# Second half of a convolution: transposes for its statistics a product later, two groups of weight sums gated at another place

## The chip, the cores and the metric

The kernel runs on one core of one Trainium2 chip. Its time is the device time of one execution in microseconds (us); the time of a kernel is the median of several executions. Engines are named as in the profile: PE (TensorE, its matmuls), DVE (VectorE), ACT (ScalarE), POOL (GpSimd) and SP (SyncE, which here only issues DMAs).

## The reference, cut to what matters

1024 tokens of 1024 channels pass two layers. Layer 0 mixes tokens with a gated linear recurrence, layer 1 with a causal Conformer convolution; each mixer is followed by a squared-ReLU MLP of 4096 hidden units, with a residual and a layer norm after each. The change lies in layer 1:

```python
def conformer_conv_mixer(h, w_pw1, b_pw1, w_dw, b_dw, ln_g, ln_b, w_pw2, b_pw2):
    u = h @ w_pw1 + b_pw1
    a, gate = jnp.split(u, 2, axis=-1)
    u = a * jax.nn.sigmoid(gate)
    u = depthwise_causal_conv(u, w_dw) + b_dw            # 31 taps per channel
    u = jax.nn.silu(layer_norm(u, ln_g, ln_b))
    return u @ w_pw2 + b_pw2
x = layer_norm(ALPHA * x + mix, ln_mix_g[1], ln_mix_b[1])
ff = jnp.square(jax.nn.relu(x @ ffn_w1[1])) @ ffn_w2[1]
x = layer_norm(ALPHA * x + ff, ln_ffn_g[1], ln_ffn_b[1])
```

## The kernel before, in words

**Products.** Every matrix is held as two float32r parts, hi and lo, with hi + lo the float32 value. `product` (L327) issues three matmuls per block of 128 input channels (hi·hi, hi·lo, lo·hi), so a product over 1024 channels is 24 matmuls of 128x512. At its end it runs one entry of the list `bg.chores` and then `bg.pump`, which hands out background work (the convolution's taps) to DVE and POOL, as far as a clock of estimated costs lets it. A scheduler then fixes the order of the instructions on every engine from a timing model; on the chip each engine takes its instructions in that order, and the SP queue its DMAs too. A weight comes as a raw tile by DMA; ACT copies it to hi, DVE subtracts to get lo (`Slots.split`, L76); `wa.ahead(n)` keeps up to n weights ready.

**Order of layer 1.** The tokens are cut in two halves of 512. The string `SEQ` (L38) gives the steps: P is the first pointwise product with gate, N the end of a half's convolution, F its norm and SiLU, S the second pointwise product with residual and norm (`second`, L1322), UA and UB the first MLP product of the first and the second half (`up_half`), V, W and X parts of the two last column sets of that product, Z the rest of these. While the second half is convolved (18 taps on DVE into a PSUM bank, 12 on POOL through products made by ACT), PE works at UA0 to UA3 and V6. F1 is spread over UA4 and UA5, S1 follows, then W6, X7 and UB0 to UB5. From V6 to W6 two PSUM banks are left for products (L1405), S1's among them.

**Statistics of the second half.** The convolution's result stays channel by channel: `by_channel(j)` is a 128x512 tile of channel block j. Its norm needs sums over channels, so after every odd j `measured` (L1207) transposes blocks j-1 and j on PE (8 transposes of 128x128 into two PSUM banks) and DVE takes `bn_stats` of them. `convolve` appends `measured` to the list `late` at the end of block j (L1234) and empties `late` at tap 10 of the next block (L1197 to L1199). The last `measured` is run by `stats` in `second_half` (L1268), which then calls `averages` (L1255): `bn_aggr` four times, plus eps on DVE, power -1/2 on POOL (L1260), minus mean times scale on DVE. A chore later `spread` (L1273) multiplies scale and minus-mean-times-scale, each broadcast, by the identity on PE, so that they lie along the free dimension in two PSUM banks. DVE then multiplies each of the eight channel blocks by the scale, POOL adds the other (L1284), ACT and DVE make SiLU and split it into `sT[1]` (the tile `xb`), which S1 multiplies. As the blocks of a pair are done, their space takes the residual back by DMA (L1296, `kept` into `y`); `second` scales it by ALPHA and adds a bias on DVE (`y<-y,b_pw`).

**Weight sums.** The MLP of layer 1 multiplies in seven forms of 2x2 blocks where there would be eight products, so some weights are sums of the four blocks of a column set. `pool_sums` (L443) loads the four blocks into a ring of four raw tiles, makes four sums on POOL (128x1024 each, every one from the one before it) and stores each to DRAM by an SP DMA. With an argument `after`, POOL first copies one column of `after` into each tile: the loads then can't start before `after` is written.

Of the kernel before, what the change touches and what calls it, by code (L numbers as in the profile page):

```python
# [8 lines left out]
F32 = mybir.dt.float32  # L9
# [6 lines left out]
P = 128  # L16
D = 1024
S = 1024
KB = D // P
# [241 lines left out]
def body(ctx, tc, d, out):  # L261
# [21 lines left out]
    def ring(kbs, shape, name, dt=F32):  # L283
        return Ring([view(kb, shape, dt, name) for kb in kbs])

    def run(kb, n, size):
        return [kb + i * size for i in range(n)]
# [4 lines left out]
    def raws(kbs, name="raw"):  # L292
        return ring(kbs, (1024,), name)

    def bank(ids):
        return Ring([banks[:, i] for i in ids])
# [18 lines left out]
    bg = Background()  # L315
# [8 lines left out]
    def aux():  # L324
        return rings["aux"]().rearrange("p (a b) -> p a b", a=NTB)
# [112 lines left out]
    def sum_place(name, layer, c):  # L438
        if (name, layer, c) not in sums:
            sums[name, layer, c] = dram.tile([4, P, 1024], F32, name=f"sum_{name}{layer}{c}")  # L440
        return sums[name, layer, c]

    def pool_sums(name, layer, c, four, after=None):  # L443

        t = sum_place(name, layer, c)
        a = {q: four() for q in (2, 3, 0, 1)}
        for q in a:
            if after is not None:
                nc.gpsimd.tensor_copy(out=a[q][:, :1], in_=after)
            nc.sync.dma_start(out=a[q], in_=d[name][layer, c, q])  # L450

        for i, (x, y) in zip((1, 0, 2, 3), ((2, 3), (0, 2), (3, 0), (0, 1))):
            nc.gpsimd.tensor_tensor(out=a[y], in0=a[x], in1=a[y], op=ALU.add)
            nc.sync.dma_start(out=t[i], in_=a[y])

    to_sum = [(*of, c) for of in (("w2", 0), ("w2", 1)) for c in range(NFC)]
# [44 lines left out]
    qn, kn, at = ([p1(n) for _ in range(2)] for n in ("qn", "kn", "at"))  # L501
# [188 lines left out]
    def half_stats(bs, yt, j):  # L690
        vector.bn_stats(bs[:, j], yt[:, j * HT : (j + 1) * HT])
# [400 lines left out]
    x2T, sT, x3T = [xa, xb], [xa, xb], [xa, None]  # L1092
# [44 lines left out]
    cs, conv, pooled, late = [None, None], [], [], []  # L1137
# [26 lines left out]
    def tap(j, i):  # L1164
        return par[:, TAP + j * TAPS + i : TAP + j * TAPS + i + 1]
# [19 lines left out]
    def by_channel(j):  # L1185
        return ct[1][:, j // 2, j % 2 * HT : (j % 2 + 1) * HT]

    def convolve(half, j, u, sums, other):

        while half > normed[0]:  # L1190
            yield WAIT
        ca = cvs()
        if gate[1]:
            nc.vector.tensor_copy(out=ca[:, :1], in_=gate[1].pop())
        nc.scalar.activation(ca, u[:, :HT], AF.Identity, bias=par[:, BDW + j : BDW + j + 1], scale=tap(j, 0))  # L1195
        for i in range(1, TAPS - NPOOL):
            if i == (10 if half else 6):  # L1197
                while late:
                    late.pop(0)()  # L1199
            vector.scalar_tensor_tensor(out=ca, in0=u[:, i : i + HT], scalar=tap(j, i), in1=ca, op0=ALU.mult, op1=ALU.add)  # L1200
            yield
        bg.flush(other)
        cb = sums["cb"]
        vector.tensor_tensor(out=by_channel(j) if half else cb, in0=ca, in1=cb, op=ALU.add)
        yield

        def measured():  # L1207

            if j == 1:
                cs[1] = stat.tile([P, NTB, 4, 6], F32, tag="cs", name="cs", bufs=1)  # L1210
            for t in range(0, NTB, 2):
                pt = rings["aux"]().rearrange("p (a b) -> p a b", a=2)
                for a in range(2):
                    for b in range(2):
                        tensor.transpose(pt[:, a, b * P : (b + 1) * P], by_channel(j - 1 + b)[:, (t + a) * P : (t + a + 1) * P], ident)
                for a in range(2):
                    vector.bn_stats(cs[1][:, t + a, j // 2], pt[:, a])

        def back():
            pt = aux()  # L1220
            for t in range(NTB):
                tensor.transpose(pt[:, t, :], cb[:, t * P : (t + 1) * P], ident)
            nc.scalar.copy(out=ct[half][:, :, j * P : (j + 1) * P], in_=pt)
            turned[0] += 1
            if j % 4 == 3:
                if j == 3:
                    cs[half] = stat.tile([P, NTB, 4, 6], F32, tag="cs", name="cs", bufs=1)[:, :, :2]
                for t in range(NTB):
                    half_stats(cs[half][:, t], ct[half][:, t, :], j // 4)

        if half:
            turned[0] += 1
        if half == 0 or j % 2:
            late.append(measured if half else back)  # L1234
# [29 lines left out]
    def second_half():  # L1264

        at = {}

        def stats():  # L1268
            while late:
                late.pop(0)()  # L1270
            at["mv"] = averages(1)

        def spread():  # L1273

            for i, name in ((3, "scale"), (4, "mean")):
                at[name] = pt = banks[:, (3, 7)[i - 3]]
                for t in range(NTB):
                    tensor.matmul(pt[:, t * P : (t + 1) * P], at["mv"][:, t, i : i + 1].to_broadcast([P, P]), ident, start=True, stop=True)
            m = big("z")
            nc.scalar.copy(out=m, in_=at["mean"])  # L1280
            for j in range(KB):
                c = by_channel(j)
                vector.tensor_tensor(out=c, in0=c, in1=at["scale"], op=ALU.mult)
                nc.gpsimd.tensor_tensor(out=c, in0=c, in1=m, op=ALU.add)  # L1284

            pool_sums(*to_sum.pop(0), raws((144, 148, 152, 161), "four"))

        def one(j):
            c, sg = by_channel(j), big("r")
            gj, bj = par[:, CLG + j : CLG + j + 1], par[:, CLB + j : CLB + j + 1]  # L1290
            nc.scalar.activation(sg, c, AF.Sigmoid, bias=bj, scale=gj)
            nc.scalar.activation(c, c, AF.Identity, bias=bj, scale=gj)
            vector.tensor_tensor(out=c, in0=c, in1=sg, op=ALU.mult)
            split(sT[1][:, 0, j, :], sT[1][:, 1, j, :], c)
            if j % 2:
                nc.sync.dma_start(out=ct[1][:, j // 2, :], in_=kept[1][j // 2])  # L1296

        nothing = lambda: None
        bg.chores += [stats, spread, nothing, *(lambda j=j: (one(j), one(j + 1)) for j in range(0, KB, 2))]

    def finish(half):
# [188 lines left out]
    for op, i in steps:  # L1490

        if op + str(i) in ("P10", "S0", "S1", "UA0", "UB0", "Z0"):
            bg.done()

        bg.hold = op in ("N", "F", "S") or bg.hold and op == "P1"
        if op == "S":
            gate[:] = sT[i][:, 1, KB - 1, :1].bitcast(F32), [ct[i][:, NTB - 1, :1]] * 2
            wa.behind = [gate[0]] * (3 if i == 0 else 0)
        bg.margin = 1e3 if op == "S" else 5.0 if op in ("N", "F") else 0.0 if op != "P1" else bg.margin
        if op in ("P0", "P1"):  # L1500
            pointwise(int(op[1]), i)
        elif op == "N":
            normalise(i)
        elif op == "F":
            if i == 1:

                rings["aux"] = bank((0, 4, 3, 7))
            second_half() if i else finish(i)
        elif op == "S":
            second(i)  # L1510
        elif op == "UA":
            up_half(1, i, 0, wa, stA, x3T[0])
        elif op in AHEAD:
            late_ahead(i, AHEAD[op])
        elif op == "Z":
            late_rest()
        else:
            if i == 0:
                wa.raws = raws((184, 188))
                drop(wa_last[1])  # L1520

                four = raws((132, 136, 140, 216), "four")
                for c in range(LATE):
                    pool_sums("w1b", 0, c, four, x3T[1][:, 1, KB - 1, 3 * P - 1 : 3 * P].bitcast(F32))
                wa.plan([form("w1b", 0, c, j) for j in LATE_ORDER for c in range(LATE)])
                stB = {"hr": ring(run(0, 2, 16), (8, 2, 256), "hb"), "r": ring(run(128, 2, 2), wide_t, "r"), "t": ring(run(112, 4, 4), (2, 2, 256), "ht")}
            if i == 2:
                x4 += ring((132, 136, 140, 216), (2, HT), "x4", F32R).views
                tmp = ring(run(176, 4, 2), wide_t, "xt")
                for k in range(4):  # L1530
                    bg.chores += x3_differences(k, tmp)
            up_half(1, i, 1, wa, stB, x3T[1])
# [98 lines left out]
```

Two calls matter here. In `spread` (L1286) a set of `w2` is summed, with no `after`. At UB0 (L1522 to L1525) the two late sets of `w1b` are summed in the same four tiles one after the other, with `after` a column of the lo part of `x3T[1]` (the tile `xc`, the normed input of UB): the last channel block, last token of token block 2 of the four that `second` makes by `norm` and `turn` (one `norm` and eight transposes per token block, then two hi and two lo splits).

## Time and profile before

| | before |
|---|---|
| median of 3 executions | 2132.28 us (2131.18 to 2132.79) |
| profiled execution, its own time | 2131.32 us |
| span of the profile | 2129.5 us |
| outside the span | 1.82 us |
| PE granted clock, mean | 0.999 |
| DMA read and written | 364.73 MB and 184.55 MB, 258 GB/s over the span |

Times in the profile count from the start of the span. A row of the timeline has start, length, engine, line of the code, operation, output and inputs, and how many equal instructions in a row it merges; in brackets the idle time before it and what ended that. Line L196 is the wrapper that all matmuls and most DVE and POOL operations go through, so operations are told apart by their tiles. The waits view has, after the colon, total us, times and the longest one.

### The profile page before, as it was taken

The numbers are of one execution on the slowest core, as the hardware profiler recorded it, in microseconds if no ns is written. First come the engines' busy times: TensorE is split into PE (matmuls) and PEld (weight loads), VectorE is DVE, ScalarE is ACT, GpSimd is POOL, SyncE is SP. The second block draws the span as 40 slices with busy tenths as digits, with TensorE's granted clock in tenths as the row PEclk, the third lists the DMA queues.
The fourth block names the chain that finished last, engine by engine and source line by source line (L and its number), as shares of the span: only waits on it lengthen the run. The fifth ranks groups of instructions, "written<-read, shape, count | busy, mean of one in ns | idle before, by whom it ended". The sixth has DMA issues, their size and how long they took to land. (4 is left out here: it accounts for less than half of the span.)

```text
span 2129.5 us, 27331 instructions
## 1 busy us (share of the span) xinstructions
PE 2108.3 (99%) x10136; PEld 1753.2 (82%) x10136; DVE 1534.3 (72%) x2208; ACT 971.4 (46%) x1370; POOL 451.5 (21%) x405
## 2 busy tenths in 40 slices
PE   8999999999999999999999999999999999999998
PEld 7888888888888888888888888888788888888887
DVE  7568898877777666656666798799957946765456
ACT  4222332232266555544444676557444445534333
POOL 0001121123100000000001599189513200040002
PEclk9999999999999999999999999999999999999999
DMA  5567867854248767899998755564585997996642
GB/s 185 144 159 175 229 178 180 232 157 176 92 144 295 268 229 258 310 372 325 339 337 308 292 193 183 208 247 168 194 299 196 335 349 263 370 341 219 192 163 99
DMA packets 166118, 500.76 MB, mean 235 GB/s; under 512 B 15840, under 2 KB 45792, under 8 KB 164704
## 3 DMA queue, kind: packets, MB, share of 16 engines
q1 hardware_dynamic: 159264, 473.85, 63.1%
q0 software_dynamic: 6720, 25.17, 6.7%
q8 instruction: 79, 1.29, 0.2%
q14 instruction: 55, 0.45, 0.1%
HBM read 364.73 MB, written 184.55 MB: 258 GB/s over the span
## 5 line engine op out<-in xcount | busy, mean ns | idle before, releaser
L196 PE MATMUL ps<-dw,dh 128*128 128x512 f32 x2688 | 611.0, 389 | 0.0
L196 PEld LDWEIGHTS ps<-dw,dh 128*128 128x128 f32 x2688 | 504.1, 188 | 104.5
L196 PE MATMUL ps<-x1f,fw 128*128 128x512 f32 x1344 | 305.3, 389 | 0.0
L196 PEld LDWEIGHTS ps<-x1f,fw 128*128 128x128 f32 x1344 | 252.1, 188 | 52.3
L196 PE MATMUL ps<-xa,wa 128*128 128x512 f32 x1152 | 267.5, 391 | 0.0
L196 PEld LDWEIGHTS ps<-xa,wa 128*128 128x128 f32 x1152 | 214.5, 188 | 44.4 <-ACT r L932 0.3
L196 POOL TENSOR_TENSOR cb<-cb,prod 128x512 f32<-128x512 f32 x176 | 234.2, 1340 | 17.8 <-ACT prod L1180 7.1
L196 DVE TENSOR_TENSOR dw<-dr,dw 128x1024 fp32r<-128x1024 f32 x112 | 141.4, 1264 | 97.2 <-ACT dw L77 94.2
L196 DVE TENSOR_TENSOR dh<-dh 128x1024 fp32r<-128x1024 f32 x112 | 140.4, 1256 | 93.7 <-ACT dh L77 93.5
L196 DVE SCALAR_TENSOR_TENSOR ps<-u,par,ps 128x512 f32<-128x512 f32 x288 | 199.6, 752 | 10.9 <-ACT ps L1195 9.4
L196 PE MATMUL ps<-x0T,wa 128*128 128x512 f32 x768 | 189.5, 399 | 6.2 <-ACT x0T L375 6.2
L77 ACT CAST dw<-dr 128x1024 fp32r<-128x1024 f32 x112 | 117.5, 1053 | 156.8 <-PE ps L196 133.8
L77 ACT CAST dh<-dh 128x1024 fp32r<-128x1024 f32 x112 | 117.1, 1050 | 124.9 <-DMA dh<-hf 124.3
L196 PEld LDWEIGHTS ps<-x0T,wa 128*128 128x128 f32 x768 | 142.9, 190 | 35.2 <-ACT x0T L375 6.2
L77 ACT CAST wa<-raw 128x1024 fp32r<-128x1024 f32 (+1 forms) x75 | 76.8, 1026 | 174.4 <-PE ps L196 118.2
L196 PE MATMUL ps<-xc,wa 128*128 128x512 f32 x672 | 153.3, 389 | 0.5 <-DVE wa L196 0.5
L1180 ACT ACTIVATE prod<-u,par 128x512 f32<-128x512 f32 x176 | 125.5, 722 | 56.3 <-POOL cb L196 55.6
L196 PEld LDWEIGHTS ps<-xc,wa 128*128 128x128 f32 x672 | 126.0, 188 | 27.5 <-DVE wa L196 1.3
L196 PE MATMUL ps<-wv,x0T 128*128 128x512 f32 x576 | 140.5, 395 | 0.0
L196 DVE TENSOR_TENSOR wa<-raw,wa 128x1024 fp32r<-128x1024 f32 (+1 forms) x75 | 96.9, 1293 | 58.4 <-ACT wa L77 54.6
L411 POOL TENSOR_TENSOR mv<-mv,nhalf 128x1 f32<-128x1 f32 x32 | 45.6, 1425 | 405.2 <-DVE mv L196 405.2
L196 PEld LDWEIGHTS ps<-wv,x0T 128*128 128x128 f32 x576 | 106.2, 188 | 21.4
(223 smaller groups left out, 2775.7 us busy)
## 6 DMA issues: line engine op xcount, KB each, us to landing
wa<-ready SPq DMA_DIRECT2D x122, 512.0 KB, 4.8
dh<-hf SPq DMA_DIRECT2D x112, 512.0 KB, 5.1
ready<-spare SPq DMA_DIRECT2D x74, 512.0 KB, 4.8
dr<-sum_w SPq DMA_DIRECT2D x64, 512.0 KB, 7.1
sum_w<-in_w_dram SPq DMA_DIRECT2D x24, 1024.0 KB, 8.9
dr<-in_w_dram SPq DMA_DIRECT2D x48, 512.0 KB, 7.6
hf<-ht SPq DMA_DIRECT2D x80, 256.0 KB, 4.1
raw<-in_w1q_dram SPq DMA_DIRECT2D x36, 512.0 KB, 4.0
```

What stands on the lines that cost most here:

```text
L77: self.nc.scalar.copy(out=slot[:, 0, c], in_=raw[:, c])
L196: return op(*args, **kw)
L411: nc.gpsimd.tensor_tensor(out=dst, in0=src, in1=nhalf[:, :n], op=ALU.pow)
L1180: nc.scalar.activation(tp, u[:, k : k + HT], AF.Copy, scale=tap(j, k))
```

## The change

Three edits.

1. At tap 10 of a block of the second half, `late` is not run but moved to the end of `bg.chores`; `product` runs it at its next end, so `measured` is issued one product later.
2. The `pool_sums` of `spread` gets `after = at["mv"][:, 0, 3:4]`, the scale that POOL's power has just made.
3. The `pool_sums` of the late sets at UB0 take as `after` the last token of token block 1 of `xc` in place of block 2.

```diff
             if i == (10 if half else 6):
+                if half:
+
+                    bg.chores += late
+                    late.clear()
                 while late:
                     late.pop(0)()
...
-            pool_sums(*to_sum.pop(0), raws((144, 148, 152, 161), "four"))
+            pool_sums(*to_sum.pop(0), raws((144, 148, 152, 161), "four"), at["mv"][:, 0, 3:4])
...
-                    pool_sums("w1b", 0, c, four, x3T[1][:, 1, KB - 1, 3 * P - 1 : 3 * P].bitcast(F32))
+                    pool_sums("w1b", 0, c, four, x3T[1][:, 1, KB - 1, 2 * P - 1 : 2 * P].bitcast(F32))
```

The program that is built from it has the same instructions on PE, DVE and ACT, and four more copies of one column on POOL.

## The prediction

> **What bounds the kernel now.** First the page: its engines and its chain.
>
> ```profile
> span 2129.5 us, 27331 instructions
> PE 2108.3 (99%) x10136; PEld 1753.2 (82%) x10136; DVE 1534.3 (72%) x2208; ACT 971.4 (46%) x1370; POOL 451.5 (21%) x405
> PE 20%; DVE 0%; DVEq 0%; issue 0%
> ```
>
> PE is busy for all but 21.2 us of the span, and no matmul is added or removed, so only PE's idle time can be won or enlarged. Next the view of waits, for PE, then the timeline of PE round each wait behind 1400 us.
>
> ```profile
> PE ps L196 <- ACT x0T L375: 6.2, 1, 6.2
> PE ps L196 <- DVE y L196: 3.0, 2, 1.9
> ...
> PE ps L196 <- DVE wa L196: 0.5, 2, 0.3
> ```
> ```profile
> 1474.55 28.14 PE L196 MATMUL ps<-xa,wa 128*128 128x512 f32 x123
> 1504.64 0.88 PE L196 MATMUL ps<-ident,y 128*128 128x128 f32 x6 [1.95 <-DVE y L196]
> ...
> 1535.96 1.16 PE L196 MATMUL ps<-ident,mv 128*128 128x128 f32 x8 [0.46 <-POOL mv L1260]
> 1538.29 1.16 PE L196 MATMUL ps<-ident,mv 128*128 128x128 f32 x8 [1.17 <-DVE mv L196]
> ...
> 1686.20 11.18 PE L196 MATMUL ps<-xc,wa 128*128 128x512 f32 x48 [0.32 <-DVE wa L196]
> 1697.55 12.80 PE L196 MATMUL ps<-xc,wa 128*128 128x512 f32 x55 [0.18 <-DVE wa L196]
> ```
>
> The largest wait (6.2) is at the kernel's start. Where the change works, PE loses 1.95 us before transposes of the statistics, 0.46 + 1.17 = 1.63 us before the matmuls that spread mean and scale, and 0.32 + 0.18 = 0.50 us in the UB steps. That is 4.08 us, or 0.19%: all that can be won. A wait made new on the path can cost more.
>
> **Part 1: transposes a product later.** Gain taken: **0**. What is issued later need not stand later, since a scheduler orders PE. Comparing the two built orders: each `measured` was split into two transposes and, later, six; counted in matmuls of UA0 to V6, the six stood behind numbers 79, 196 and 349, and in the changed program they stand behind 79, 196 and 349 again. Only the first two, which read the earlier block, go back (from 24 to 48, from 105 and 107 to 120, from 220 and 226 to 240). The 1.95 us is that of the six behind number 349; what ends it is the last add of block 5:
>
> ```profile
> 1503.91 0.68 DVE L196 TENSOR_TENSOR y<-ps,cb 128x512 f32<-128x512 f32 x1
> ```
>
> DVE's order is the same up to there, so the add ends at 1504.59 and the wait stays. Bounds: 0 to 1.95 won; I take 0, because the order says so.
>
> **Part 2: the sums of `w2` gated by the scale.** Gain: **1.63**. POOL and DVE before:
>
> ```profile
> 1530.05 4.87 POOL L453 TENSOR_TENSOR four<-four 128x1024 f32<-128x1024 f32 x2 [20.81 <-DVE cs L196]
> 1534.88 1.03 POOL L1260 TENSOR_TENSOR mv<-mv,nhalf 128x4 f32<-128x4 f32 x1
> 1541.60 12.33 POOL L1284 TENSOR_TENSOR y<-y,z 128x512 f32<-128x512 f32 x8
> ```
> ```profile
> 1531.02 1.46 DVE L196 TENSOR_SCALAR mv<-mv 128x4 f32<-128x4 f32 x1
> 1535.94 2.29 DVE L196 SCALAR_TENSOR_TENSOR mv<-mv 128x4 f32<-128x4 f32 x1 [3.46 <-POOL mv L1260]
> ```
>
> The power had its input at 1532.48 but stood behind two weight sums until 1534.88. The tiny DVE instruction behind it then took 2.29 us, as long as the weight sum that POOL had begun at its side. In the changed order POOL has the power, four one-column copies, one sum, two `y<-y,z`, a sum, six `y<-y,z`, two sums. The power ends near 1533.5 at the latest and DVE's instruction meets copies alone, so both are done before PE arrives at 1535.5. Both waits go.
>
> What is late next is S1. The four loads now leave at 1532.5 or later, so the first sum, ahead of every `y<-y,z`, starts near 1538 to 1540 (5.1 to 7.3 us behind the copies, by rows of part 3) and ends near 1541 to 1542: the first `y<-y,z` comes when it did (1541.60). The second sum delays the last six by about 2.5 us, and the last two sums now run at the side of DVE's SiLU products, which POOL slows:
>
> ```profile
> 1551.00 3.48 DVE L196 TENSOR_TENSOR y<-y,r 128x512 f32<-128x512 f32 x2
> 1563.27 1.29 DVE L196 TENSOR_TENSOR y<-y,r 128x512 f32<-128x512 f32 x2
> 1564.64 1.30 DVE L196 TENSOR_TENSOR xb<-y,xb 128x512 fp32r<-128x512 f32 x2
> 1565.97 1.23 DVE L196 SCALAR_TENSOR_TENSOR y<-y,b_pw 128x1024 f32<-128x1024 f32 x1
> 1570.56 1.22 DVE L196 SCALAR_TENSOR_TENSOR y<-y,b_pw 128x1024 f32<-128x1024 f32 x1 [3.37 <-DMA y<-kept]
> 1575.80 0.69 DVE L196 TENSOR_TENSOR y<-y,ps 128x512 f32<-128x512 f32 x1 [4.02 <-PE ps L196]
> ```
> ```profile
> 1567.44 39.84 PE L196 MATMUL ps<-wa,xb 128*128 128x512 f32 x175
> ```
>
> 1.74 us each with POOL at work, 0.65 without. With POOL busy to about 1562 in place of 1554, some four such instructions lose 1.1 us each, so the last split of `xb` ends near 1570.5, not 1565.94. S1 (1.63 earlier: 1565.8) reads the last two channel blocks in its matmuls 31 to 36, from 1572.6 at 39.84 / 175 = 0.228 us each: in time. But the last `kept` load leaves only after that split and its residual was ready 4.6 us later (1565.97 to 1570.56), so `y<-y,b_pw` ends near 1576.4, where 4.02 us of slack stood before `y<-y,ps`. S1 has two PSUM banks; `y<-y,ps` (0.69) must have read the first before matmul 49, at 1576.8, and now ends at 1577.1 if four DVE instructions are slowed, at 1579.3 if six are. With three there would be no wait: 0 to 2.5 us, and I take **+0.7**. On SP the stores of the sums stand between the weights of S1: the last of its first four goes behind the third store, near 1560, and is needed at 1572; no cost.
>
> **Part 3: the late sets' sums a token block sooner.** Cost: **+1.6**. A gate moved forward puts work ahead of something: in POOL's order the copies and first sum now stand before the power of token block 3.
>
> ```profile
> 1618.29 1.52 POOL L411 TENSOR_TENSOR mv<-mv,nhalf 128x1 f32<-128x1 f32 x1 [5.97 <-DVE mv L196]
> 1622.40 0.54 POOL L449 COPY four<-xc 128x1 f32<-128x1 f32 x4 [2.58 <-DVE xc L196]
> 1629.73 2.40 POOL L453 TENSOR_TENSOR four<-four 128x1024 f32<-128x1024 f32 x1 [6.80 <-DMA four<-in_w1b_dram]
> ```
> ```profile
> 1611.83 1.28 DVE L196 TENSOR_TENSOR xc<-ps,xc 128x512 fp32r<-128x512 f32 x2
> 1619.85 1.28 DVE L196 SCALAR_TENSOR_TENSOR y<-y,mv,ln_mix_b 128x1024 f32<-128x1024 f32 x1 [0.44 <-POOL mv L411]
> 1652.14 3.42 DVE L196 TENSOR_TENSOR ht<-hb 128x1024 f32<-128x1024 f32 x1
> ```
> ```profile
> 1624.53 1.03 PE L196 MATMUL ps<-ident,y 128*128 128x128 f32 x8
> ```
> ```profile
> 482.80 0.83 POOL L449 COPY four<-yn 128x1 f32<-128x1 f32 x4 [8.46 <-DVE yn L196]
> 487.94 9.83 POOL L453 TENSOR_TENSOR four<-four 128x1024 f32<-128x1024 f32 x4 [4.30 <-DMA four<-in_w_dram]
> ...
> 1858.26 0.54 POOL L449 COPY four<-y 128x1 f32<-128x1 f32 x4 [194.81 <-ACT dh L77]
> 1868.73 11.39 POOL L453 TENSOR_TENSOR four<-four 128x1024 f32<-128x1024 f32 x4 [9.93 <-DMA four<-in_w_dram]
> ```
> ```profile
> 1613.00:1616.00 3.00, 3.00 (x15) 2.49 (x14) 3.00 (x5) 1.01 (x1) 0.00 (x0) 1.00 0.00 0
> ```
>
> Block 1's split ends at 1613.11, so the copies start near 1613.2. From first copy to first sum the trace has 5.1, 7.3 (1622.40 to 1629.73) and 10.5 us; the stretches row shows no DMA at 1613 to 1616, so I take 5.1: the sum runs 1618.3 to 1620.7, the power to 1622.2 instead of 1619.81. Then DVE's `ln_mix_b` meets the second sum: 3.42 us, the row of a 1024-column DVE instruction beside a sum, so `y` is there at 1625.7 and not 1621.13. Its transposes are due at 1624.53: 1.1 us of waiting, 2.2 if DVE's `ln_mix_g` just before holds the first sum up by as much again. Between, +1.6. Bounds: 0 (if DVE goes first: 1.28 us, ready at 1623.5) and 6.5 (10.5 us for the loads). Behind the waiting `ln_mix_b` stand, on DVE, one split of block 2, a weight and block 3's splits, due when PE begins UB0 two products later; the weight is for UB0's third product; both have room. On SP, raw weights now stand behind the first set's stores and the second set's first loads, 1 to 5 us later than before; the first of them is for UB0's fourth product, which PE reaches 20 us after.
>
> The Trainium skill (SBUF — State Buffer, Who interferes with whom) says that a DVE instruction with two SBUF inputs and a POOL instruction that reads SBUF exclude each other for a whole instruction, whichever starts first. By that rule `ln_mix_b` would take 2.40 + 1.28 = 3.7 us and the sum would be 0.3 higher, or, with DVE first, this part would cost nothing; the 2.29 us above agree with the first.
>
> For this the second set's sums, which slow DVE in the UB steps, come some 10 us sooner:
>
> ```profile
> 1652.04 11.41 POOL L453 TENSOR_TENSOR four<-four 128x1024 f32<-128x1024 f32 x4 [2.23 <-DMA four<-in_w1b_dram]
> 1676.57 1.23 DVE L196 TENSOR_TENSOR ht<-hb 128x1024 f32<-128x1024 f32 x1
> ```
>
> 3.42 against 1.23 us for the same instruction: this is how DVE fell behind with the weights that PE waits for at 1686 and 1697. Sooner, the slow stretch lies over fewer queued instructions: I take **-0.5**, bounds -0.5 and +2.2 (one more instruction at 3.42).
>
> **Sum.** -1.63 + 0.7 + 1.6 - 0.5 = +0.2 us on the profiled execution (2131.32, of it 2129.5 span). It lies 0.96 under the median, 2132.28; against the median the forecast is **2132.5 us**: no change.
>
> **Rivals.**
> - *Part 3 costs nothing:* the loads land faster or DVE goes first; -1.63 + 0.7 - 0.5 = -1.4, or -2.1 if S1 isn't late either: 2130.2 to 2130.9. For it: DMAs idle before. Against: the 2.29 us row, where POOL went first.
> - *Slower: the power of block 3 behind late loads.* At 10.5 us the sum starts at 1623.7, the power ends at 1627.6, `y` is ready at 1631.0: 6.5 us lost, in all +5.1, 2137.4. It decides from 9.5 us on. For it: the loads at 1858. Against: four loads are alone here.
> - *Part 1 does what it says:* 1.95 more won, at best 2128.2. Against it: the unchanged place of the six.
> - *DVE's new order in the UB steps starves PE of weights* there for some us: up to 2136. Against: DVE has fewer slowed instructions.
>
> **How the numbers follow.** Forecast 0.58 (2131.5 to 2134.5), part 3 free 0.24, slower by late loads 0.08, part 1 works 0.04, starved 0.06. Low end: all gains without part 1 give 2130.2, less 0.8 for the spread of the runs, 2129.4. High end: +2.5 for S1 and +3.3 for part 3 (7.3 us for the loads), with -1.63 and -0.5, give 2136.0, with the spread 2136.8. 0.2% is 4.3 us, about what a measurement of this kernel can tell from no change: even all gains stay inside, so faster 0.03; slower 0.10 (late loads, and some of the starved case); same 0.87.
>
> **What would show it.** Right: no wait before `ps<-ident,mv`; 1.95 us still before the six transposes; POOL's sum before the last `mv` power of S1, and a new wait of 1 to 2 us before the transposes of `y` near 1623; no wait for `wa` in UB2 and UB3. Wrong: S1's matmuls waiting for `xb` or for a weight behind a store; a wait before UB0 for `xc`; or no transposes' wait at 1503.

## The result, and the profile after

| | before | after |
|---|---|---|
| median of the runs side by side (13 each) | 2132.29 us (2129.56 to 2137.42) | 2138.34 us (2134.20 to 2143.80) |
| profiled execution, its own time | 2131.32 us | 2140.92 us |
| span of the profile | 2129.5 us | 2139.1 us |

The ratio after to before is 1.0028, with a 95% interval of 1.0019 to 1.0037: the changed kernel is **slower by 0.28%**, 6.05 us between the medians. The forecast was 2132.5 us with a range up to 2136.8; the time lies above it. Of the runs further below, one of edit 2 alone took 4686.01 us, more than twice any other, and is left out of its row.

First the page of after, its span and engines, and its view of PE's waits (total us, times, longest).

```profile
span 2139.1 us, 27341 instructions
PE 2110.4 (99%) x10136; PEld 1755.0 (82%) x10136; DVE 1538.9 (72%) x2208; ACT 972.0 (45%) x1370; POOL 455.3 (21%) x409
```
```profile
PE ps L196 <- ACT x0T L375: 6.2, 1, 6.2
PE ps L196 <- ACT r L932: 5.3, 2, 3.7
PE ps L196 <- DVE y L196: 4.1, 2, 2.2
PE ps L196 <- DVE qn L196: 2.2, 2, 1.9
PE ps L196 <- DVE state L196: 1.9, 2, 1.7
```

PE is busy 2.1 us longer and idle 7.5 us more. The row that stood in no list of before is the second: PE waits 5.3 us for ACT. The waits for `mv` and for `wa` are gone, as forecast. The timeline of PE round the change, in after:

```profile
1507.90 0.87 PE L196 MATMUL ps<-ident,y 128*128 128x128 f32 x6 [1.89 <-DVE y L196]
...
1538.38 1.95 PE L196 MATMUL ps<-ident,mv 128*128 128x128 f32 x16
...
1559.10 5.75 PE L196 MATMUL ps<-xa,wa 128*128 128x512 f32 x24 [1.51 <-ACT r L932]
1568.60 7.31 PE L196 MATMUL ps<-xa,wa 128*128 128x512 f32 x24 [3.74 <-ACT r L932]
1575.74 39.84 PE L196 MATMUL ps<-wa,xb 128*128 128x512 f32 x175
...
1635.19 1.09 PE L196 MATMUL ps<-ident,y 128*128 128x128 f32 x8 [2.20 <-DVE y L196]
1636.04 5.71 PE L196 MATMUL ps<-xa,wa 128*128 128x512 f32 x24
```

Such starts, taken from both timelines, divide the 9.6 us between the two profiled executions:

| stretch | before | after | difference |
|---|---|---|---|
| span's start to the six transposes of part 1 | 1504.64 | 1507.90 | +3.26 |
| from there to S1 | 62.80 | 67.84 | **+5.04** |
| S1 to the transposes of token block 3 | 57.09 | 59.45 | **+2.36** |
| from there to the end | 504.97 | 503.91 | -1.06 |

The +3.26 isn't the change's: it comes from waits for `qn` and `state` in layer 0, which are 4.1 us in this execution and 0.8 in that of before; and this execution is 2.6 us above its median. The other three rows make +6.3, about the 6.05 between the medians.

Why PE waits for ACT: the products of UA4 and UA5 use two PSUM banks, and `r<-ps` (L932) on ACT empties them, one per product of 24 matmuls. Behind it in the same queue, and before it, stand the sigmoids and casts of the SiLU. The timeline of ACT in after:

```profile
1558.47 0.57 ACT L932 ACTIVATE r<-ps 128x512 f32<-128x512 f32 x1
...
1566.21 0.62 ACT L675 CAST xb<-y 128x512 fp32r<-128x512 f32 x1 [4.00 <-DVE y L196]
1566.73 0.81 ACT L1295 ACTIVATE r<-y,par 128x512 f32<-128x512 f32 x1
1567.45 0.60 ACT L675 CAST xb<-y 128x512 fp32r<-128x512 f32 x1
1567.96 0.58 ACT L932 ACTIVATE r<-ps 128x512 f32<-128x512 f32 x1
```

and in before:

```profile
1555.76 0.57 ACT L932 ACTIVATE r<-ps 128x512 f32<-128x512 f32 x1
...
1560.62 0.57 ACT L932 ACTIVATE r<-ps 128x512 f32<-128x512 f32 x1
```

In before two of these emptyings lie 4.9 us apart, in after 9.5, while PE fills a bank in 5.5 us (24 at the 19.10 us that 83 of the same matmuls took). Between them ACT stands 4.00 us at a cast that needs DVE's `y<-y,r`. Who made that late is seen on DVE and POOL in after:

```profile
1558.81 4.58 DVE L196 TENSOR_TENSOR xb<-y,xb 128x512 fp32r<-128x512 f32 x2
1563.31 3.46 DVE L196 TENSOR_TENSOR y<-y,r 128x512 f32<-128x512 f32 x2
...
1584.10 0.69 DVE L196 TENSOR_TENSOR y<-y,ps 128x512 f32<-128x512 f32 x1 [3.68 <-PE ps L196]
...
1631.75 3.38 DVE L196 SCALAR_TENSOR_TENSOR y<-y,mv,ln_mix_b 128x1024 f32<-128x1024 f32 x1 [2.62 <-POOL mv L411]
```
```profile
1549.78 10.24 POOL L1288 TENSOR_TENSOR y<-y,z 128x512 f32<-128x512 f32 x6
1559.99 5.63 POOL L453 TENSOR_TENSOR four<-four 128x1024 f32<-128x1024 f32 x2
...
1621.55 2.59 POOL L449 COPY four<-xc 128x1 f32<-128x1 f32 x4 [0.93 <-DVE xc L196]
1628.81 2.40 POOL L453 TENSOR_TENSOR four<-four 128x1024 f32<-128x1024 f32 x1 [4.67 <-DMA four<-in_w1b_dram]
1631.18 0.54 POOL L411 TENSOR_TENSOR mv<-mv,nhalf 128x1 f32<-128x1 f32 x1
1631.69 9.04 POOL L453 TENSOR_TENSOR four<-four 128x1024 f32<-128x1024 f32 x3
```

These four DVE instructions take 8.04 us, at the side of POOL's last two sums of `w2` (the first of them still beside an add); pairs of them without POOL took 1.29 and 1.30 us in before. The chain of the longer wait, 3.74 us, is: sums on POOL, SiLU on DVE, cast on ACT, emptying of a bank behind the cast, PE.

The shorter wait, 1.51 us, is of another kind: the last two sums began only behind it, at 1559.99. The emptying that ends it was no later than in before: counted from the six transposes it began after 50.57 us, in before after 51.12. But PE, rid of the waits for `mv`, came for the bank after 49.69 us already. So most of what edit 2 won was waited for here.

At 1584.10 DVE itself waits 3.68 us for PE: S1's residual, which the prediction held to be late next, was in time, for an S1 that began late.

The longer wait has a tail: the 24 matmuls behind it take 7.31 us in place of 5.5. The windows view of after (stretch, PE's busy time and starts, granted clock, DMA share, GB/s) shows why:

```profile
1567.00:1567.50 0.50, 0.00 (x0) 1.00 1.01 385
...
1571.00:1571.50 0.50, 0.50 (x3) 0.50 0.94 369
...
1572.00:1572.50 0.50, 0.50 (x3) 1.00 1.02 418
```

The granted clock is 0.50 until about 1572 and 1.00 again from there.

### The profile page after: what moved, and what is told of

It reads as the page before. It is cut to its first block, busy times and chain, and to the rows that moved or that the text cites. A ratio compares the mean times of both kernels' runs of the same rounds, so it can differ in the third digit from the quotient of the medians.

```text
span 2139.1 us, 27341 instructions
## 1 busy us (share of the span) xinstructions
PE 2110.4 (99%) x10136; PEld 1755.0 (82%) x10136; DVE 1538.9 (72%) x2208; ACT 972.0 (45%) x1370; POOL 455.3 (21%) x409
## 3 DMA queue, kind: packets, MB, share of 16 engines
q8 instruction: 79, 1.29, 0.2%
## 4 chain that ended last, share of the span: by engine, by line
PE 88%; DMA 3%; POOL 3%; DVE 3%; issue 1%; ACT 1%; SPq 0%; DVEq 0%; POOLq 0%
PE ps L196 88%; POOL cb L196 3%; DMA sum_w<-in_w_dram 1%; DVE y L196 1%; DMA raw<-in_wg_dram 1%; DVE ps L196 1%; DVE wa L196 0%; DVE xb L196 0%; DMA raw<-in_wv_dram 0%; DMA sum_w<-sum_w 0%; DMA four<-in_w_dram 0%; DMA raw<-in_wqf_dram 0%; DMA four<-in_w1b_dram 0%; DMA raw<-in_xT_dram 0%; POOL four L449 0%
## 5 line engine op out<-in xcount | busy, mean ns | idle before, releaser
L196 DVE TENSOR_TENSOR dh<-dh 128x1024 fp32r<-128x1024 f32 x112 | 144.7, 1295 | 90.5 <-ACT dh L77 84.1
```

The lines of the kernel that those rows point to most:

```text
L196: return op(*args, **kw)
```

## The experiments

Theory behind them: PE waits for ACT because POOL's last two `w2` sums slow the SiLU on DVE; the rest is block 3's wait. Main rivals: the loads and stores of the moved sums, or the transposes of part 1. "Distance" below is from the six transposes of part 1 to S1 (before: 62.80). Each ratio is to runs of before that were made side by side with the kernel; their median was 2133.34 us for the three single edits and the gate at the norm's last add, 2132.12 for the gate behind the last split and for before with four banks, 2133.18 for the others.

| kernel | median us, runs | ratio to before, 95% interval | distance |
|---|---|---|---|
| edit 1 alone | 2132.07, 11 | 0.9998, 0.9989 to 1.0007 | 62.7 |
| edit 2 alone | 2137.26, 10 | 1.0017, 1.0008 to 1.0027 | 67.4 |
| edit 3 alone | 2134.76, 11 | 1.0009, 1.0000 to 1.0019 | 62.8 |
| edit 2, gate at the norm's last add | 2135.84, 11 | 1.0015, 1.0006 to 1.0024 | 62.0 |
| edit 2, gate behind the last split | 2136.41, 12 | 1.0014, 1.0004 to 1.0025 | 62.0 |
| edit 2, two of the sums left out | 2135.0, 1 | | 62.0 |
| edit 2 and four banks | 2135.47, 11 | 1.0017, 1.0009 to 1.0026 | 62.0 |
| before and four banks | 2134.67, 12 | 1.0007, 0.9997 to 1.0017 | 62.5 |
| before, late sets' gate at block 3's power | 2136.76, 11 | 1.0014, 1.0005 to 1.0023 | 64.3 |
| edit 3, one sum in the first set | 2132.43, 1 | | 64.3 |

In the last two rows the granted clock fell to 0.50 near 1540, behind waits for `mv` of 0.60 and 1.17 us, which their edits don't touch; this is where the 1.5 us of distance come from.

**Edit 1 alone.**

```diff
+                if half:
+                    bg.chores += late
+                    late.clear()
                 while late:
```

> Edit 1 alone (measured goes through the list of chores). Theory: the scheduler puts the six transposes that wait for the last add at the same place, so nothing changes: 2132 us, within 0.1% of before, with the wait of 1.9 us before six transposes of y near 1505 still there. Rival (edit 1 shares in the loss, by the later first two transposes or by chores that are pushed back behind it): 2 us or more slower, with a new wait in UA or in S1.

No change that can be measured. The wait is where it was; PE's timeline:

```profile
1504.28 0.87 PE L196 MATMUL ps<-ident,y 128*128 128x128 f32 x6 [1.89 <-DVE y L196]
1504.91 20.69 PE L196 MATMUL ps<-xa,wa 128*128 128x512 f32 x83
```

The 83 matmuls take 20.69 us here and 19.10 in after: the granted clock was 0.50 at 1506 to 1509. PE reached the spread of mean and scale later by as much and waited 0.28 us there, where before waited 1.63. So what this fall costs is nearly all taken out of the wait that edit 2 removes.

**Edit 2 alone.**

```diff
-            pool_sums(*to_sum.pop(0), raws((144, 148, 152, 161), "four"))
+            pool_sums(*to_sum.pop(0), raws((144, 148, 152, 161), "four"), at["mv"][:, 0, 3:4])
```

> Edit 2 alone (the sums of w2 gated by the scale). Theory: the 1.6 to 2.1 us before the spreading matmuls go, but POOL's first sum waits for its loads ahead of the first adds of the norm, and the second sum stands ahead of the other six; ACT, which must empty the two PSUM banks of UA4 and UA5, waits in order behind the SiLU of blocks that aren't there yet, so PE waits 5 us on ACT in UA4 and UA5 and loses 7 us there in all: about +5 us, 2137. Rival A (SP: weights behind the stores of the sums): the same time, but PE waits for wa or a DMA, not for ACT's r. Rival B (the loss needs edits 1 or 3 too): 2130 to 2132.

It carries most of the loss. PE's timeline has both waits for ACT and the slow product:

```profile
1555.84 5.74 PE L196 MATMUL ps<-xa,wa 128*128 128x512 f32 x24 [1.07 <-ACT r L932]
1565.34 7.29 PE L196 MATMUL ps<-xa,wa 128*128 128x512 f32 x24 [3.77 <-ACT r L932]
```

**Edit 3 alone.**

```diff
-                    pool_sums("w1b", 0, c, four, x3T[1][:, 1, KB - 1, 3 * P - 1 : 3 * P].bitcast(F32))
+                    pool_sums("w1b", 0, c, four, x3T[1][:, 1, KB - 1, 2 * P - 1 : 2 * P].bitcast(F32))
```

> Edit 3 alone (the late sets' sums gated by token block 1). Theory: POOL's power of token block 3 stands behind the first sum and its loads, DVE's last norm instruction behind it meets the second sum: PE waits about 2.2 us before the transposes of block 3, and gains the 0.5 us of waits for wa in UB2 and UB3: +1.7 us, 2134, with the waits before the spreading matmuls (1.6 us) as before. Rival (that wait comes from the w2 sums or S1 being late, not from this gate): no wait before these transposes and 2131.8.

The wait before block 3's transposes comes with this edit; the waits for `wa` in UB go with it.

```profile
1630.58 1.09 PE L196 MATMUL ps<-ident,y 128*128 128x128 f32 x8 [2.11 <-DVE y L196]
```

The three ratios, -0.02%, +0.17% and +0.09%, add to 0.24%; all three edits together gave 0.28%. Inside the intervals they add up.

**Are the last two sums the cause?** Of the four sums of that `w2` set the third and fourth are left out. The loads and all four stores stay; two of the stores then write blocks that aren't summed.

```diff
-    def pool_sums(name, layer, c, four, after=None):
+    def pool_sums(name, layer, c, four, after=None, n=4):
...
-        for i, (x, y) in zip((1, 0, 2, 3), ((2, 3), (0, 2), (3, 0), (0, 1))):
+        for m, (i, (x, y)) in enumerate(zip((1, 0, 2, 3), ((2, 3), (0, 2), (3, 0), (0, 1)))):
+            if m < n:
...
-            pool_sums(*to_sum.pop(0), raws((144, 148, 152, 161), "four"))
+            pool_sums(*to_sum.pop(0), raws((144, 148, 152, 161), "four"), at["mv"][:, 0, 3:4], 2)
```

> Edit 2 alone, but the third and fourth sum of that w2 set are left out (their stores write unsummed blocks, so those weights are wrong); the first two stand among the norm's adds as with edit 2. Theory, first form (ACT's queue is held by DVE, which the last two sums slow at the side of its SiLU products): the long wait of PE on ACT in UA5 (3.8 us) goes, the first one (1.1) stays; from the six transposes near 1505 to S1's start 63 us and not 67.4. Second form (the first two sums, ahead of the norm's adds, are what is late): both waits stay, 67 us.

Both waits for ACT are gone: PE runs from the spread to S1 (at 1571.60) without a gap. On PE, and the two emptyings on ACT:

```profile
1543.37 28.39 PE L196 MATMUL ps<-xa,wa 128*128 128x512 f32 x124
1571.60 18.75 PE L196 MATMUL ps<-wa,xb 128*128 128x512 f32 x82
```
```profile
1558.65 0.58 ACT L933 ACTIVATE r<-ps 128x512 f32<-128x512 f32 x1
...
1564.03 0.59 ACT L933 ACTIVATE r<-ps 128x512 f32<-128x512 f32 x1
```

The emptyings lie 5.4 us apart, in edit 2 alone 9.5 (1555.21 and 1564.70), and the four DVE instructions that take 8.05 us there take 3.76 here. Loads and stores were the same in number, so it is the two sums that make the longer wait. The shorter one was expected to stay, and that it went says nothing of these sums: the emptying that ends it in edit 2 alone begins before they do. In this profile the clock fell ahead of the spread, so PE came to the bank 1.6 us later, while the emptying began 49.06 us behind the six transposes and not 50.12; that is enough. The single time, 2135.0, holds a wait of 3.9 us that ends at 247 us and has nothing to do with the edit; it says little.

**Is the bank the resource?** Edit 2 with four PSUM banks in place of two for the products from `spread` to S1.

```diff
-        nothing = lambda: None
+        def nothing():
+            rings["mm"] = bank((1, 5, 0, 4))
...
+        if half == 1:
+            rings["mm"] = bank((1, 5))
```

> Edit 2 alone, with four PSUM banks in place of two for the products of UA4 and UA5 that follow the spreading matmuls (the banks of the finished statistics); S1 has its two again. Theory (PE waits because two banks are full while ACT's queue stands): no wait of PE on ACT's r in UA4 and UA5, the spreading waits gone: from the six transposes to S1's start 60 to 61 us, 2130 to 2131, unless S1 then finds its last splits late (up to 5 us at its start or middle, on DVE xb). Rival (the delay is that of the SiLU itself, needed by S1): the same 67 us, moved into a wait before or in S1, and 2137.

The sums stay beside the SiLU, ACT stands 4.18 us at a cast and two of its emptyings lie 9.7 us apart (1555.44 and 1565.12), and yet no matmul waits for it: with two banks, this stall of the queue was the bottleneck. (The clock fell ahead of the spread in this profile too, so the shorter wait isn't tested.) The distance, 62.0, is above the 60 to 61 that was expected, by the 1.6 us of that fall. But now S1 starts on time and is itself too early. Its rows on PE, SP's DMAs ahead of them, and the instruction on DVE that the first of these waits for:

```profile
1571.33 0.47 PE L196 MATMUL ps<-wa,xb 128*128 128x512 f32 x1 [0.40 <-DMA wa<-ready]
1573.04 6.85 PE L196 MATMUL ps<-wa,xb 128*128 128x512 f32 x29 [1.24 <-DMA wa<-ready]
1581.20 28.86 PE L196 MATMUL ps<-wa,xb 128*128 128x512 f32 x126 [1.31 <-DVE y L196]
```
```profile
1562.04 0.32 SPq L1296 DMA_DIRECT2D y<-kept  x1
...
1562.93 0.38 SPq L454 DMA_DIRECT2D sum_w<-four  x1
1563.41 2.68 SPq L86 DMA_DIRECT2D wa<-ready  x2
1566.18 1.13 SPq L454 DMA_DIRECT2D sum_w<-four  x1
...
1567.92 1.16 SPq L86 DMA_DIRECT2D wa<-ready  x2
```
```profile
1556.32 5.70 DVE L196 TENSOR_TENSOR xb<-y,xb 128x512 fp32r<-128x512 f32 x2
```

S1 waits 1.64 us for weights and 1.31 us for the residual. The weights left SP late: until 1562.04 the queue stood 8.6 us at a load of the residual, `y<-kept`, whose space is free only behind DVE's slowed split of `xb`; two stores stood among the weights behind it. What the stores add was not separated. The late residual is what the prediction expected; in after, PE's wait for ACT hides both.

**The four banks without edit 2**, to see whether they make S1 late by themselves.

> The kernel before with nothing changed but the PSUM banks of the products in UA4 and UA5: four after spread in place of two. It tells what made S1 wait in the run with four banks and edit 2 (2.95 us there: 1.64 for weights behind stores, 1.31 for the residual). Theory: the sums of w2 that edit 2 puts off cause both, so here S1 has none of these waits; the two mv waits of the kernel before (together about 1.6) stay, no matmul waits for ACT r, the distance from the six transposes to S1 stays 62.6 to 63.0, and the time is that of before, ratio 0.999 to 1.001. Rival: the ring of four banks or the order that it brings makes S1 late, so the waits of 1.2 and 1.3 are here as well and the ratio is 1.001 to 1.002.

```profile
1566.63 11.04 PE L196 MATMUL ps<-wa,xb 128*128 128x512 f32 x48
1578.01 28.86 PE L196 MATMUL ps<-wa,xb 128*128 128x512 f32 x126 [0.33 <-DVE y L196]
```

0.33 us for the residual, none for weights. So of the 2.95 us, at least 2.6 come from edit 2's later sums and stores. The rival falls.

**Two later gates for the `w2` sums**, so that none runs among the norm's adds, or none beside the SiLU:

```diff
-            pool_sums(*to_sum.pop(0), raws((144, 148, 152, 161), "four"))
+            pool_sums(*to_sum.pop(0), raws((144, 148, 152, 161), "four"), by_channel(KB - 1)[:, :1])
```

> Edit 2 with another gate: the loads of the w2 sums wait for the norm's last add on POOL (block 7), so that POOL has the power and the eight adds first and then the four sums; no edits 1 and 3. The stores of the sums still stand among the weights of S1 on SP. Theory: the waits before the spreading matmuls go (-2 us) and PE doesn't wait for ACT in UA4 and UA5, since the SiLU isn't held up: 2130, unless the sums, now at the side of DVE's splits and in the space that the normed tokens of S1 go to, hold up S1's end or the transposes of its last token blocks, which the program now has closer to UB0 (a wait there of up to 5 us). Rival A (SP: weights behind the stores): a loss of several us stays, and PE waits for wa or a DMA in UA5 or S1.

```diff
-            pool_sums(*to_sum.pop(0), raws((144, 148, 152, 161), "four"))
...
+            if j == KB - 1:
+                pool_sums(*to_sum.pop(0), raws((144, 148, 152, 161), "four"), sT[1][:, 1, j, :1].bitcast(F32))
```

> Edit 2 with another gate: the sums of w2 start only behind DVE's last split of xb, so that POOL does none beside the SiLU products of the second half. Theory: no wait for mv and none for ACT r; the distance from the six transposes to S1 is 61.0 to 62.0 (1 to 1.7 us less than before); what this gains is given back in the UB steps, since PE's order there is the one of the version gated by the norm's last add (2 to 4 us of waits for wa there), or in S1 by weights whose loads stand on SP behind the gated ones: ratio 1.000 to 1.002. Rival: the waits in UB came from the sums' place and not from PE's order; then there are none, and with 1.6 us won the time is 2131 to 2132, ratio 0.999 to 0.9995.

Both have no wait for `mv`, none for ACT's `r` and none in S1, and start S1 0.8 us sooner than before although in both profiles the clock fell near 1506, which cost 1.6 us. But the scheduler gave both another order of the later transposes, and in both the weights came late in the UB steps, the hi parts of ACT and the lo parts of DVE. PE in the kernel with the gate behind the split:

```profile
1698.38 0.73 PE L196 MATMUL ps<-xc,wa 128*128 128x512 f32 x2 [1.32 <-ACT wa L77]
1699.85 5.72 PE L196 MATMUL ps<-xc,wa 128*128 128x512 f32 x24 [0.74 <-DVE wa L196]
1706.79 33.39 PE L196 MATMUL ps<-xc,wa 128*128 128x512 f32 x146 [1.23 <-DVE wa L196]
```

3.29 us there, 3.29 with the other gate (1.17, 0.74, 1.20 and 0.18), 0.50 in before. What was won ahead of S1 is given back; of the gate at the last add 2130 us had been expected. Whether the order of the transposes or that of DVE's own queue starves PE was not separated.

**A gate between the two:** the late sets wait for the power of token block 3. POOL's copies then start 1.59 us behind the start of that power; in before they start 4.11 us behind it, with edit 3 ahead of it.

```diff
+    rstd = []
...
         mu, rs = moments(yt)
+        rstd[:] = [rs]
...
-                    pool_sums("w1b", 0, c, four, x3T[1][:, 1, KB - 1, 3 * P - 1 : 3 * P].bitcast(F32))
+                    pool_sums("w1b", 0, c, four, rstd[0])
```

> Before, with the late sets' sums gated by the power of token block 3 itself (POOL's last mv), some 3 us sooner than before and behind the power in POOL's order. Theory (edit 3 costs because the first sum and its loads stand ahead of that power): no wait of PE before the transposes of block 3, the waits for wa in UB2 and UB3 gone or no more than 0.5 us: 2132, same as before or 0.5 better. Rival (any sums at the side of block 3's norm cost it): 1 to 2 us of waiting there, 2134.

As expected there is no wait before block 3's transposes. Not expected was one of 2.06 us in the UB steps, with a fall of the clock behind it:

```profile
1685.22 35.05 PE L196 MATMUL ps<-xc,wa 128*128 128x512 f32 x146 [2.06 <-DVE wa L196]
```

The gate of before is the best of the three that were tried.

**What makes block 3 late?** Edit 3 with only the first of four sums made in the first late set, the other three left out (`n` as above; the stores stay).

```diff
-                    pool_sums("w1b", 0, c, four, x3T[1][:, 1, KB - 1, 3 * P - 1 : 3 * P].bitcast(F32))
+                    pool_sums("w1b", 0, c, four, x3T[1][:, 1, KB - 1, 2 * P - 1 : 2 * P].bitcast(F32), 1 if c == 0 else 4)
```

> Edit 3 alone, but of the first late set only the first sum is made (the other three are left out and unsummed blocks stored, so those weights are wrong). POOL still has that sum and its loads ahead of the power of block 3. If the 2.1 us before block 3's transposes are the price of the power being late, they stay; if what costs is DVE's last norm instruction at the side of the second sum (3.4 in place of 1.3 us), the wait falls to 0.2 us or less.

On PE and on DVE:

```profile
1626.55 1.09 PE L196 MATMUL ps<-ident,y 128*128 128x128 f32 x8 [0.56 <-DVE y L196]
```
```profile
1625.21 1.28 DVE L196 SCALAR_TENSOR_TENSOR y<-y,mv,ln_mix_b 128x1024 f32<-128x1024 f32 x1 [3.09 <-POOL mv L411]
```

Without a second sum at its side `ln_mix_b` takes 1.28 us, not 3.38, and the wait is 0.56, not 2.11. The 2.10 us between 3.38 and 1.28 are the whole wait of edit 3 alone. The 0.56 that stays goes with the loads: from the first copy to the first sum it was 7.72 us here (1614.55 to 1622.27) and 7.18 in edit 3 alone (1617.02 to 1624.20). So the late power uses up the slack that `ln_mix_b` had, and the second sum at its side makes the wait.

## Why the prediction was wrong, step by step

- **Part 1 at 0: right.** The six transposes stood where they were, with 1.89 us before them.
- **Part 2, -1.63: right in mechanism.** Both waits for `mv` went. Its size was read from one execution, though: in six of twelve profiles the clock fell shortly ahead of it (between 1505 and 1515), and in edit 1 and edit 3 alone, where it did so, the wait was 0.28 and 0.36.
- **Part 2, "What is late next is S1", +0.7: this step failed.** The prediction followed the slowed SiLU along DVE and SP to S1, and left ACT's queue out. Late next was ACT's `r<-ps`, behind casts that wait for that SiLU: 1.51 + 3.74 = 5.25 us of waiting and 1.8 more (7.31 less 5.5) at half clock. With -1.63 that is +5.4 against -0.93 on record; the distance to S1 says +5.04, and the 0.4 between is spread over neighbouring rows, most of it at the spread, whose 16 matmuls no longer start twice after a wait. The longer wait is shown from both ends: without the last two sums the emptyings lie 5.4 us apart and not 9.5, and with four banks the stalled queue holds up no matmul. That the shorter one is the gain of edit 2, waited for at a bank that came free no sooner, is read from the traces of before and after and was not tested. DVE and POOL had been priced well: less the 3.26 us by which this execution stands later, POOL's last sum ended at 1562.36 (about 1562 in the prediction) and the last split of `xb` at 1570.53 (1570.5).
- **S1's weights on SP, "no cost": wrong as well, but hidden.** With four banks they cost 1.64 us and the residual 1.31. The prediction looked at the stores alone; the queue stood 8.6 us at a load of the residual ahead of them.
- **Part 3, +1.6: right place and mechanism, too small.** 2.20 us in after, 2.11 alone. From the first copy to the first sum it was 7.3 us and not 5.1; the power then took 0.54 us behind the sum and not 1.52; `ln_mix_b` took 3.38, as priced (3.42). The first two misses have opposite signs, +2.2 and -1.0, so the size came out nearer than its terms. On the point where the Trainium skill (SBUF — State Buffer, Who interferes with whom) gave another sum, 3.7 us for `ln_mix_b`, the trace has 3.38 where the sum began 0.06 us ahead of it, and 1.28 where none ran: nearly the whole exclusion that the page states.
- **-0.5 for the waits in UB: right.** None is left in after.
- **Rivals.** The one on the slow side needed loads of 9.5 us; they took 7.3, and it didn't happen. The loss came by a way that was no rival; the 0.10 for slower had other reasons.

## What to carry to other kernels

When background work moves beside an engine, follow the slowed instructions into every in-order queue that waits for them, and ask above all which of those queues frees a resource with only two buffers: here ACT's emptying of two PSUM banks stood behind casts whose result PE needed only later. Time that PE wins ahead of such a bank is won only if the bank comes free sooner too. A wait of PE of about 2 us or more should be priced with the half clock that can follow it, 1.6 to 1.8 us here. A wait that is removed counts only for the executions that have it; see in more than one profile whether it is there.

## What the runs showed of the hardware

The granted clock can fall to 0.50 after a PE wait well below 3 us. The wait before the six transposes was 1.86 to 1.98 us in all twelve profiles; the clock fell behind it in six and not in the other six:

| 83 matmuls behind it | wait of that profile, us |
|---|---|
| 20.68 to 20.72 us (clock fell) | 1.89 (edit 1), 1.98 (edit 3), 1.96 and 1.92 (later gates), 1.86 (two sums), 1.97 (edit 2 and banks) |
| 19.08 to 19.10 us | 1.95 (before), 1.89 (after), 1.97 (edit 2), 1.96 (power), 1.86 (one sum), 1.89 (before and banks) |

So the length of the wait doesn't decide it in this range. The price is 1.6 us each time. After the waits of 3.74 and 3.77 us it fell both times, from PE's restart for about 3.4 us (1568.60 to 1572.0 in after). The Trainium skill (TensorE: Matmul & The Clock Gate, Part 1: The HAM clock gate) says that the clock halves after an idle window of some 3.4 us and comes back after as long of sustained work, counted in a window that runs by itself. The time to come back agrees; that nearly 3.4 us of idleness are needed does not, since 1.9 us were enough in half of the profiles. Nor does the length decide above 2 us: behind the 2.20 us in after it did not fall (24 matmuls in 5.71 us), behind the 2.11 us in edit 3 alone (7.31 us) and the 2.06 us in the UB steps it did. Shorter waits in a row can do it too: it fell behind 0.60 and 1.17 us with 1.2 us of small matmuls between them in two profiles, and not behind 0.46 or 0.44 and 1.17 us in two others. That the phase of such a window decides would fit, and no run here tests it.
